# Transposing a head's two weight tiles together into two-bank PSUM tiles, and adding the causal mask on VectorE

## The chip, the cores and the metric

The kernel runs on one NeuronCore of a Trainium2 chip. The metric is the device time of one launch in microseconds (us). A core has five engines that run side by side and meet at semaphores: TensorE (PE in the profile; its weight loads are PEld), VectorE (DVE), ScalarE (ACT), GpSimd (POOL) and SyncE (SP), which only issues transfers. PSUM, the memory into which TensorE writes, has eight banks of 512 float32 values per partition; ScalarE and VectorE read it, GpSimd does not.

## The reference

One layer of a streaming encoder for 1024 prompt frames and 64 sample frames, width 1024, all in float32. What the change touches is the attention of the prompt, in two branches of eight heads (64 wide):

```
h = RMSNorm(x);  q, k, v of both branches, f, gate = h @ w_in;  q, k normalised per head
A: each 64-frame chunk reads itself and the 8 chunks before it
   p = softmax(q.k / 8 + bias[head, distance]);        o_a = p @ v
B: causal, c = cumsum(log sigmoid(f + b_f)) per head
   p = softmax(q.k / 8 + c[t] - c[s], s <= t);         o_b = p @ v
x = x + (sigmoid(gate_a) * (o_a @ w_pa) + sigmoid(gate_b) * (o_b @ w_pb)) @ w_o
x = x + experts(RMSNorm(x))     (32 experts, two of them per frame)
```

## The kernel before, in words

The frames are nine tiles of 128 (the last one holds the 64 sample frames). Every float32 product is made of float32r matmuls on a high and a low part, so a value that a matmul reads is first split: ScalarE copies it to float32r (the high part), VectorE subtracts that from the value (the low part).

The first 620 us or so are eight passes, one for each pair of heads: pairs 0 to 3 of branch A, then 0 to 3 of branch B. In a pass (`qkv`) TensorE projects the nine tiles with 24 matmuls a tile, and between these matmuls the attention of the pair is worked in, in four query groups `g` of 256 frames (two tiles `j` of 128), for two heads `h`. After it come gates, merges and the sample's heads, the output projection, and the experts, whose weights stream from HBM.

One head of one group goes like this. `scores(j)` multiplies q with up to 1024 keys into one or two PSUM tiles `big`; VectorE adds the bias (branch A) or `S = bias - c` (branch B) and keeps a running minimum (L598); ScalarE takes the exponential (L536), VectorE the reciprocal of the sum (L538), ScalarE scales (L540). In branch B one more bf16 matmul, identity times `tribig`, adds the causal mask to the last 128 columns. `weights(j, u)` transposes up to four 128x128 blocks of S (`tr`, L95) into a one-bank PSUM tile `small`; ScalarE copies it into `PT` as the high part (L635), VectorE subtracts for the low part (L636). So a tile j with more than four blocks in its group takes two such calls, u = 0 and 1. `values` then multiplies v with PT into another `small`. `turn_qk` transposes the normalised q and k of the next pair of frame tiles (`raw`) into a `small` too; three ScalarE instructions (L470, L474 twice) and two of VectorE (L475) read that one.

The order on TensorE is fixed by hand. Each call is put into a queue with a due time, either a number of ticks (a tick is three projection matmuls) or a time on a clock that the planner advances by its own estimate of TensorE's work (`late`). `D_W0 = 8` is the distance from a tile's scores to its first transposes, `D_W1 = 1.2` that from u = 0 to u = 1, `D_VAL = 4.5` that to `values`. TensorE takes its instructions strictly in that order: one that waits holds all behind it. Which buffer of a pool a tile gets, and the order on the other engines, a scheduler decides when the kernel is built. PSUM has two pools of four one-bank buffers: `big` (NBIG) and `small` (NSMALL). A tile of a pool can be written when the last reader of its buffer's former tile is done.

Of the kernel before, what the change touches and what calls it, by code (L numbers as in the profile page):

```python
# [24 lines left out]
CAP = 96  # L25
NOV = 22
EPS = 1e-6
NBIG, NSMALL = 4, 4
O_TURN, O_LOG, O_RANK, O_TAB = 3, 4, 7, 3
SA, SB, PTA, PTB, NORM_POOL, D_NORM, ATT0, ATT1, WPOOL, WR, SS, WO_EVERY, PF, SQ, FOX_POOL, V_POOL, RC_ACT, KT, NX, NN, NU0, E0, YB = 4, 3, 2, 1, 2, 0, 2, 26, 0, 4, 1, 3.5, 3, 2, 0, 2, 2, 1, 10, 1, 8, -1, 3  # L30
PA, PF2, HOLD_G, HELD, WARM0, XG, OT, HXB = 8, 2, -1, 1, 11, 3, 2, 1
# [4 lines left out]
NW, FPAIR, D_TURN, H_NORM, H_TURN, GRP = 16, 1, 10, 0, 4, 2  # L36
D_W0, D_W1, D_VAL, PACE = 8, 1.2, 4.5, 4.5
SL = [(0, 384), (384, 384), (768, 320)]
# [8 lines left out]
class K:  # L47
# [139 lines left out]
    def turn_h(self, i, k0):  # L187
        nc, x, n = self.nc, self.xs[i], rows(i)
        ps = self.pp.tile([128, 4, 128], F32, name="small", bufs=NSMALL)
# [74 lines left out]
    def forget(self):  # L264
# [45 lines left out]
        def sums():  # L310
            pc = self.pp.tile([128, 2, 104], F32, name="small", bufs=NSMALL)
            lff = lf.rearrange("p i h -> p (i h)")
# [13 lines left out]
        def store():  # L326
            pn = self.pp.tile([104, 128], F32, name="small", bufs=NSMALL)
# [242 lines left out]
    def scores(self, br, p, g, h, j, T, bias, G, H):  # L570
# [13 lines left out]
        if br == 1:  # L584
            (nc.gpsimd if FOX_POOL else nc.vector).tensor_scalar(
                S[:, :n], bias[h][:, :n], self.cc[:, i, 2 * p + h:2 * p + h + 1], None, op0=OP.subtract)
        pcs = self.pieces(n)
        for x, (o, m) in enumerate(pcs):
            ps = self.pp.tile([128, 512], F32, name="big", bufs=NBIG)
            ks = slice(128 * kb0 + o, 128 * kb0 + o + m)  # L590
            qs = slice(128 * j, 128 * j + 128)
            last = br == 1 and x == len(pcs) - 1
# [12 lines left out]
    def weights(self, br, p, g, h, j, T, G, H, u):  # L605

        nc = self.nc
        b0, nb = self.blocks(br, g)
        i = 2 * g + j
        kb0 = max(0, i - 4) if br == 0 else 0  # L610
        if u == 0:
            if nb > 4:
                self.late(D_W1, self.weights, br, p, g, h, j, T, G, H, 1)
        if j == 1 and u == (nb > 4):
            self.late(D_VAL, self.values, br, p, g, h, T, G, H)
        if ("PT", u) not in H:
            m, bufs = (2, self.pt_bufs) if u == 1 and nb == 6 else (4, 2)
            PT = H["PT", u] = self.ap_.tile([128, 2, m, 256], F32R, name=f"PT{m}", bufs=bufs)
            for b, jj in ((2 * g + 1, 0), (b0, 1)) if br == 0 and g >= 2 else ((2 * g + 1, 0),):
                uu, r = divmod(b - b0, 4)  # L620
                if uu == u:
                    nc.gpsimd.memset(PT[:, :, r, 128 * jj:128 * jj + 128].bitcast(F32), 0.0)
        PT = H["PT", u]
        r0, r1 = kb0 - b0, i - b0
        a, b = max(r0, 4 * u), min(r1, 4 * u + 3)
        if a > b:
            return
        S = H["S", j]
        pt = self.pp.tile([128, 4, 128], F32, name="small", bufs=NSMALL)
        for r in range(a, b + 1):  # L630
            c = (r - r0) * 128
            self.tr(pt[:, r - 4 * u, :], S[:, c:c + 128], self.ident)
        sr = slice(a - 4 * u, b + 1 - 4 * u)
        hi = PT[:, 0, sr, 128 * j:128 * j + 128]
        nc.scalar.copy(hi, pt[:, sr, :])  # L635
        nc.vector.tensor_tensor(PT[:, 1, sr, 128 * j:128 * j + 128], pt[:, sr, :], hi.bitcast(F32), op=OP.subtract)  # L636

    def values(self, br, p, g, h, T, G, H):
# [3 lines left out]
        at = G["at"]  # L642
        po = self.pp.tile([128, 256], F32, name="small", bufs=NSMALL)
        for r in range(nb):
            u, rr = divmod(r, 4)
            for hl in range(2):
                self.mm(po, T["v"][(b0 + r) // 4][:, (b0 + r) % 4, h, :], H["PT", u][:, hl, rr, :],
                                 start=(r == 0 and hl == 0), stop=(r == nb - 1 and hl == 1))
# [22 lines left out]
    def sample2(self, br, p, P, rk, rv, qk, qh, ql):  # L671
        nc, I = self.nc, self.I
        pt = self.pp.tile([128, 4, 128], F32, name="small", bufs=NSMALL)
        for i in range(4):
# [6 lines left out]
        def head(h):  # L681
# [15 lines left out]
            if br == 1:  # L697
                nc.vector.tensor_scalar(S, bias[:, :576], self.cc[:64, 12, hd:hd + 1], None, op0=OP.subtract)
            for x, o in enumerate((0, 288)):
                ps = self.pp.tile([128, 512], F32, name="big", bufs=NBIG)  # L700
                sl = slice(o, o + 288)
                last = br == 1 and x == 1
                self.mm(ps[:64, :288], qh[:, h], ks[h][:, sl], start=True, stop=False)
                self.mm(ps[:64, :288], ql[:, h], ks[h][:, sl], start=False, stop=not last)
                if last:
                    self.mm(ps[:64, 224:288], self.identb[:64, :64], self.tribig[:64, :64],
                                     start=False, stop=True)
                add = bias[:, sl] if br == 0 else S[:, sl]
# [6 lines left out]
        def weights(h, V, S):  # L715
            pt = self.pp.tile([128, 5, 64], F32, name="small", bufs=NSMALL)
            for i in range(5):
# [10 lines left out]
        def values(h, V, PT):  # L728
            rw = slice(64 * h, 64 * h + 64)
            po = self.pp.tile([128, 256], F32, name="small", bufs=NSMALL)  # L730
            for i in range(5):
# [168 lines left out]
    def out_tile(self, i, mh, ml):  # L900
# [5 lines left out]
        def turn(k0):  # L906
            pt = self.pp.tile([128, 4, 128], F32, name="small", bufs=NSMALL)
            for k in range(4):
# [28 lines left out]
        def logits():  # L937
            pl = self.pp.tile([128, 40], F32, name="small", bufs=NSMALL)
            for k in range(8):
# [67 lines left out]
    def place(self, i, n, OH, E):  # L1007

        nc = self.nc
        V = nc.vector  # L1010
        pp = self.pp.tile([128, 32], F32, name="small", bufs=NSMALL)
        for j in range(2):
# [58 lines left out]
    def turn(self, xg):  # L1071
# [3 lines left out]
        for k0 in (0, 4):  # L1075
            pt = self.pp.tile([128, 4, CAP], F32, name="small", bufs=NSMALL)
            for k in range(4):
# [4 lines left out]
    def hidden(self, u, xT):  # L1082
        nc = self.nc
        ph = self.pp.tile([128, 2, CAP], F32, name="small", bufs=NSMALL)
        for j in range(2):
# [73 lines left out]
    def overflow(self):  # L1159
# [7 lines left out]
        self.placed = None  # L1167
        pc = self.pp.tile([128, 32], F32, name="small", bufs=NSMALL)
        for j in range(2):
# [69 lines left out]
    def run(self):  # L1239
# [178 lines left out]
```

## Time and profile before

| | us |
|---|---|
| median of 3 runs (1242.94 to 1246.67) | 1245.81 |
| the profiled execution, device time | 1241.81 |
| its span, first to last instruction | 1240.0 |
| TensorE busy in the span | 1190.5 (96%) |
| VectorE, ScalarE, GpSimd busy | 788.6, 740.9, 314.9 |

Of the profiled execution 1.8 us lie outside its span. In a view by windows each row is a stretch, with the busy time of every engine and the number of instructions in brackets; TensorE's granted clock (PEclk, 1.00 is 2.4 GHz) stands behind. A view of groups gives count, total and mean time of instructions of one line and shape, and what the engine waited for before them. Records of matmuls overlap, since they are pipelined: how fast TensorE goes is read from the distance of the starts.

### The profile page before, as it was taken

What the parts mean: (1) busy time and instruction counts of PE and PEld (TensorE: products, weight loads), DVE (VectorE), ACT (ScalarE), POOL (GpSimd) and SP (SyncE); (2) the same over time, 40 slices, a digit from 0 to 9 for tenths busy, and PEclk for the clock granted to TensorE, in tenths of its full rate; (3) what the DMA queues carried; (4) which work ended last, traced back from release to release, by engine and by line L of the source; (5) the groups of instructions that cost most, each with busy time, mean ns of one, the idle gap of its engine ahead of it and who ended that gap; (6) DMA issues with size and microseconds to landing.
All of it is one profiled execution on the core that took longest, in us unless ns stands there. A gap on an engine that the chain in (4) does not pass through costs nothing. (4 is left out here: it accounts for less than half of the span.)

```text
span 1240.0 us, 22375 instructions
## 1 busy us (share of the span) xinstructions
PE 1190.5 (96%) x7677; PEld 1105.5 (89%) x7677; DVE 788.6 (64%) x2412; ACT 740.9 (60%) x1730; POOL 314.9 (25%) x469
## 2 busy tenths in 40 slices
PE   8999999999999999999999999999999989999993
PEld 6999999999889999899899889999988859999983
DVE  5667776767388887967467686318644444666543
ACT  5789998989498898988566443423233322333331
POOL 2643435352433434100000000000000013445421
PEclk9999999999999999999999999999999998999988
DMA  8112121222322131411233332214584458999995
GB/s 283 50 61 80 44 73 52 71 65 71 69 66 73 53 84 35 81 53 32 73 92 116 104 91 75 88 33 132 199 292 161 159 195 251 302 288 285 287 290 137
DMA packets 102538, 156.31 MB, mean 126 GB/s; under 512 B 13581, under 2 KB 77941, under 8 KB 102389
## 3 DMA queue, kind: packets, MB, share of 16 engines
q1 hardware_dynamic: 92789, 124.43, 32.6%
q0 software_dynamic: 7168, 21.50, 8.1%
q10 hardware_dynamic: 2464, 8.91, 1.9%
q8 instruction: 61, 1.00, 0.3%
q14 instruction: 56, 0.46, 0.1%
HBM read 122.08 MB, written 38.23 MB: 129 GB/s over the span
## 5 line engine op out<-in xcount | busy, mean ns | idle before, releaser
L83 PE MATMUL big<-w,hTh 128*128 128x384 f32 (+1 forms) x1152 | 324.3, 354 | 1.6 <-ACT hTh L193 0.7
L83 PEld LDWEIGHTS big<-w,hTh 128*128 128x128 f32 x1152 | 204.6, 189 | 6.2 <-DVE w L234 1.0
L83 PE MATMUL big<-hTh,w 128*128 128x384 f32 (+1 forms) x768 | 205.7, 336 | 0.0
L83 PE MATMUL big<-w,hTl 128*128 128x384 f32 (+1 forms) x512 | 173.6, 339 | 0.9 <-DVE hTl L194 0.9
L83 PEld LDWEIGHTS big<-hTh,w 128*128 128x128 f32 x768 | 138.6, 189 | 1.2
L83 PE MATMUL big<-hTl,w 128*128 128x384 f32 (+1 forms) x384 | 126.4, 329 | 0.0
L636 DVE TENSOR_TENSOR PT<-small,PT 128x512 fp32r<-128x512 f32 (+2 forms) x192 | 98.9, 520 | 21.1 <-ACT PT L635 19.2
L536 ACT ACTIVATE S<-S,mns 128x640 f32<-128x640 f32 (+7 forms) x128 | 94.3, 737 | 26.3 <-DVE mns L598 25.3
L83 PE MATMUL big<-ath,w 128*128 128x384 f32 (+1 forms) x384 | 99.4, 335 | 0.0
L540 ACT ACTIVATE S<-S,rc 128x640 f32<-128x640 f32 (+7 forms) x128 | 94.0, 736 | 7.8 <-DVE rc L538 6.9
L83 PEld LDWEIGHTS big<-w,hTl 128*128 128x128 f32 x512 | 97.0, 190 | 1.3 <-DVE hTl L194 1.2
L95 PE MATMUL small<-ident,S 128*128 128x128 f32 x528 | 89.3, 273 | 4.7 <-ACT S L540 2.6
L635 ACT CAST PT<-small 128x512 fp32r<-128x512 f32 (+2 forms) x192 | 85.1, 448 | 11.3 <-PE small L95 6.7
L83 PE MATMUL small<-PT,v 128*128 128x256 f32 x608 | 83.5, 283 | 0.0
L411 POOL TENSOR_TENSOR ssr<-ssa,mhalf 128x8 f32<-128x8 f32 (+1 forms) x40 | 61.2, 1531 | 72.6 <-DVE ssa L410 55.9
L83 PEld LDWEIGHTS small<-PT,v 128*128 128x128 f32 x608 | 79.3, 188 | 0.1
L83 PE MATMUL big<-wo,mh 128*128 128x512 f32 x288 | 75.9, 402 | 0.0
L95 PEld LDWEIGHTS small<-ident,S 128*128 128x128 f32 x528 | 65.0, 140 | 10.2 <-ACT S L540 3.8
L83 PEld LDWEIGHTS big<-hTl,w 128*128 128x128 f32 x384 | 72.9, 190 | 0.0
L83 PEld LDWEIGHTS big<-ath,w 128*128 128x128 f32 x384 | 69.0, 190 | 1.4
L83 PE MATMUL big<-k,qh 128*128 128x320 f32 (+3 forms) x192 | 64.4, 339 | 3.2 <-DVE mns L598 3.2
L449 POOL TENSOR_TENSOR v<-raw,v 128x128 fp32r<-128x128 f32 x64 | 31.2, 487 | 133.3 <-DVE v L448 125.9
(259 smaller groups left out, 2568.9 us busy)
## 6 DMA issues: line engine op xcount, KB each, us to landing
uo<-in_w SPq DMA_DIRECT2D x43, 512.0 KB
ux<-in_w SPq DMA_DIRECT2D x30, 512.0 KB
ur<-in_w SPq DMA_DIRECT2D x23, 512.0 KB
wraw<-in_w_pair SPq DMA_DIRECT2D x56, 192.0 KB
wraw<-in_w_in SPq DMA_DIRECT2D x32, 192.0 KB
atd<-at SPq DMA_DIRECT2D x32, 128.0 KB
bias<-ccd SPq DMA_DIRECT2D x8, 512.0 KB
y<-in_x_prompt SPq DMA_DIRECT2D x8, 512.0 KB
```

The source lines that it names most:

```text
L83: self.nc.tensor.matmul(out, a, b, start=start, stop=stop)
L95: self.nc.tensor.transpose(out, a, ident)
L411: nc.gpsimd.tensor_tensor(r[:n, :4 * c], a[:n, :4 * c], self.mhalf[:n, :4 * c], op=OP.pow)
L449: (nc.gpsimd if V_POOL & 2 else nc.vector).tensor_tensor(V[:, i, :, 64:128], src, V[:, i, :, 0:64].bitcast(F32), op=OP.subtract)
L536: nc.scalar.activation(S[:nq, :n], S[:nq, :n], AF.Exp, bias=mn[:nq], scale=-1.0, accum_out=sm[:nq])
L540: nc.scalar.activation(S[:nq, :n], S[:nq, :n], AF.Copy, scale=rc[:nq])
L635: nc.scalar.copy(hi, pt[:, sr, :])
L636: nc.vector.tensor_tensor(PT[:, 1, sr, 128 * j:128 * j + 128], pt[:, sr, :], hi.bitcast(F32), op=OP.subtract)
```

## The change

Five things are done together.

- `small` is split off into a pool of its own. During the eight passes it holds two tiles `turn` of two banks each (NTURN = 2) in place of four of one bank. `turn_h`, `turn_qk` and two small steps of the forget gate use it as well. After the passes it is opened again with four one-bank `small`.
- `weights` is called once for a head, 7 units after the scores of its second tile (D_W0 = 7). It transposes all blocks of tile 0 into one `turn`, all blocks of tile 1 into another, and each is read by one ScalarE copy (now L627) and one VectorE subtraction (L628). D_W1 is gone. PT is one tile for all blocks: two buffers in branch A, one in branch B.
- `values` writes into a `big`.
- The mask matmul is gone. VectorE makes `S = bias - c` for all but the last 128 columns as before, and for the last 128 one instruction makes `bias - c + tribig` (L592).
- Branch B has four S buffers in place of three, and one low part of q (`ql`) in place of two.

```diff
-NBIG, NSMALL = 4, 4
+NBIG, NSMALL, NTURN = 4, 4, 2
-SA, SB, ... = 4, 3, ...
+SA, SB, ... = 4, 4, ...
-D_W0, D_W1, D_VAL, PACE = 8, 1.2, 4.5, 4.5
+D_W0, D_VAL, PACE = 7, 4.5, 4.5
...
+    def turned_tile(self, k):
+        return self.ps_.tile([128, 8, 128], F32, name="turn", bufs=NTURN)[:, :k]
...
     def turn_qk(...):
-        pt = self.pp.tile([128, 2, 2, 128], F32, name="small", bufs=NSMALL)
+        pt = self.turned_tile(4).rearrange("p (j i) t -> p j i t", j=2)
...
     def open_ap(self, br):
-        self.q_lows(self.ap_, 256, 2)
+        self.q_lows(self.ap_, 256, 2 - br)
...
     def scores(...):
         if br == 1:
-            (nc.gpsimd if FOX_POOL else nc.vector).tensor_scalar(
-                S[:, :n], bias[h][:, :n], self.cc[:, i, 2 * p + h:2 * p + h + 1], None, op0=OP.subtract)
+            c = self.cc[:, i, 2 * p + h:2 * p + h + 1]
+            if i:
+                nc.vector.tensor_scalar(S[:, :n - 128], bias[h][:, :n - 128], c, None, op0=OP.subtract)
+            nc.vector.scalar_tensor_tensor(S[:, n - 128:n], bias[h][:, n - 128:n], c, self.tribig,
+                                           op0=OP.subtract, op1=OP.add)
...
-            self.mm(ps[:, :m], ql[:, h, qs], K[:, ks], start=False, stop=not last)
-            if last:
-                self.mm(ps[:, m - 128:m], self.identb, self.tribig, start=False, stop=True)
+            self.mm(ps[:, :m], ql[:, h, qs], K[:, ks], start=False, stop=True)
...
-        self.late(D_W0, self.weights, br, p, g, h, j, T, G, H, 0)
+        if j == 1:
+            self.late(D_W0, self.weights, br, p, g, h, T, G, H)
...
+    def weights(self, br, p, g, h, T, G, H):
         nc = self.nc
         b0, nb = self.blocks(br, g)
+        self.late(D_VAL, self.values, br, p, g, h, T, G, H)
+        PT = H["PT"] = self.ap_.tile([128, 2, self.wide // 128 + 1 - br, 256], F32R, name="PT", bufs=self.pt_bufs)
...
+        for j in range(2):
+            i = 2 * g + j
+            kb0 = max(0, i - 4) if br == 0 else 0
+            r0, n = kb0 - b0, i + 1 - kb0
+            S = H["S", j]
+            pt = self.turned_tile(n)
+            for r in range(n):
+                self.tr(pt[:, r, :], S[:, 128 * r:128 * r + 128], self.ident)
+            hi, lo = (PT[:, x, r0:r0 + n, 128 * j:128 * j + 128] for x in range(2))
+            nc.scalar.copy(hi, pt)
+            nc.vector.tensor_tensor(lo, pt, hi.bitcast(F32), op=OP.subtract)
     def values(...):
-        po = self.pp.tile([128, 256], F32, name="small", bufs=NSMALL)
+        po = self.pp.tile([128, 512], F32, name="big", bufs=NBIG)[:, :256]
...
-            self.close("ap", "tp")
+            self.close("ap", "tp", "ps")
+            self.ps_ = self.open("ps", 1, PSUM)
```

The sample's heads lose their mask matmul in the same way; the other lines of the diff only name the new pool.

How the change moves instructions on TensorE is seen at two places. A number behind a name tells one buffer's tile from the next; the brackets name the engines on whose semaphores an instruction waits. First, branch A, pair 1, group 2, second head. Before, the first three blocks of its second tile (small_2468), then the q and k of the next frame tiles (small_2474), then, after three projection matmuls, the last two blocks (small_2494):

```order
L95 MATMUL small_2468<-ident_72,S_2313 128x128 [waits PE_49]
L95 MATMUL small_2468<-ident_72,S_2313 128x128 x2
L95 MATMUL small_2474<-ident_72,raw_2178 128x128 [waits DVE_49,PE_49,Pool_49]
L95 MATMUL small_2474<-ident_72,raw_2178 128x128 [waits Pool_49]
L95 MATMUL small_2474<-ident_72,raw_2178 128x128 x2
L83 MATMUL big_2388<-w_1675,hTh_91 128x384
L83 MATMUL big_2487<-w_1525,hTh_91 128x384
L83 MATMUL big_2487<-w_1525,hTl_92 128x384
L95 MATMUL small_2494<-ident_72,S_2313 128x128 [waits DVE_49]
L95 MATMUL small_2494<-ident_72,S_2313 128x128
```

Now, the five blocks of tile 0 (turn_2418), the five of tile 1 (turn_2426) and the q and k (turn_2434) stand without anything between them:

```order
L83 MATMUL big_2361<-w_1621,hTh_91 128x384
L99 MATMUL turn_2418<-ident_72,S_2225 128x128 x5
L99 MATMUL turn_2426<-ident_72,S_2285 128x128 [waits Activation_49]
L99 MATMUL turn_2426<-ident_72,S_2285 128x128 x4
L99 MATMUL turn_2434<-ident_72,raw_2145 128x128 [waits DVE_49,Pool_49]
L99 MATMUL turn_2434<-ident_72,raw_2145 128x128 [waits Pool_49]
L99 MATMUL turn_2434<-ident_72,raw_2145 128x128 x2
L83 MATMUL big_2361<-w_1639,hTh_91 128x384
```

There are two `turn` buffers, so turn_2434 has the buffer of turn_2418; the wait on DVE in front of it is for the subtraction that reads turn_2418, five transposes earlier.

Second, branch B, pair 1, group 3, second head, its second tile. Before, the mask matmul and the eight blocks in two halves with projection between them:

```order
L83 MATMUL big_6661<-tribig_82,identb_80 128x128
L95 MATMUL small_6671<-ident_72,S_6531 128x128 [waits DVE_49]
L95 MATMUL small_6671<-ident_72,S_6531 128x128 x3
L83 MATMUL big_6568<-w_6215,hTh_91 128x384
L83 MATMUL big_6568<-w_6215,hTl_92 128x384
L83 MATMUL big_6568<-w_6218,hTh_91 128x384
L83 MATMUL big_6568<-w_6221,hTh_91 128x384
L83 MATMUL big_6691<-w_6070,hTh_91 128x384
L83 MATMUL big_6691<-w_6070,hTl_92 128x384
L95 MATMUL small_6705<-ident_72,S_6531 128x128 [waits DVE_49]
L95 MATMUL small_6705<-ident_72,S_6531 128x128 x3
```

Now, seven blocks of tile 0 and at once the eight of tile 1:

```order
L83 MATMUL big_6403<-w_6066,hTh_91 128x384
L99 MATMUL turn_6494<-ident_72,S_6302 128x128 [waits PE_49]
L99 MATMUL turn_6494<-ident_72,S_6302 128x128 x6
L99 MATMUL turn_6504<-ident_72,S_6373 128x128 [waits DVE_49,PE_49]
L99 MATMUL turn_6504<-ident_72,S_6373 128x128 x7
L83 MATMUL big_6403<-w_6081,hTh_91 128x384
L83 MATMUL big_6525<-w_5926,hTh_91 128x384
L83 MATMUL big_6525<-w_5926,hTl_92 128x384
```

Here the scheduler has put both tiles, turn_6494 and turn_6504, into the same two banks, and the wait on DVE in front of the second is for the subtraction that reads the first. Such a pair in one buffer stands at 13 of the 64 heads (five with 1 block in tile 0, three with 3, three with 5, two with 7), and q and k right behind both tiles of a head, as in the first place, seven times, all in branch A.

## Rows read from the trace of the kernel before

**Rows 1.** The page's first part: busy time of each engine.
```profile
PE 1190.5 (96%) x7677; PEld 1105.5 (89%) x7677; DVE 788.6 (64%) x2412; ACT 740.9 (60%) x1730; POOL 314.9 (25%) x469
```

**Rows 2.** Stretches, one per pass of a pair: span, busy by engine, clock, DMA.
```profile
184.00:246.00 62.00, 61.39 (x407) 59.84 (x406) 44.77 (x139) 56.02 (x133) 26.50 (x45) 1.00 0.20 60
...
459.00:528.00 69.00, 66.79 (x448) 62.96 (x447) 57.04 (x173) 62.38 (x150) 20.25 (x34) 1.00 0.26 59
...
sum 537.00, PE 526.93 PEld 501.48 DVE 402.11 ACT 465.30 POOL 185.07; mean PE 65.87 PEld 62.69 DVE 50.26 ACT 58.16 POOL 23.13
```

**Rows 3.** TensorE's waits, 31 to 620 us: for whom, us, times, longest.
```profile
PE big L83 <- DVE mns L598: 3.2, 4, 1.8
PE small L95 <- ACT S L540: 2.6, 3, 1.8
...
PE small L95 <- ACT qk L464: 1.0, 1, 1.0
PE small L95 <- DVE PT L636: 1.0, 2, 0.6
```

**Rows 4.** Timeline of TensorE, branch B: start, us, instruction.
```profile
438.16 0.34 PE L83 MATMUL big<-w,hTl 128*128 128x384 f32 x1
438.34 0.34 PE L83 MATMUL big<-w,hTh 128*128 128x384 f32 x1
...
440.95 0.23 PE L83 MATMUL big<-tribig,identb 128*128 128x128 bf16 x1
440.99 0.59 PE L83 MATMUL big<-w,hTh 128*128 128x384 f32 x2
441.42 0.34 PE L83 MATMUL big<-w,hTl 128*128 128x384 f32 x1
```

**Rows 5.** Groups by shape, 31 to 620 us: count, busy us, mean ns, idle before.
```profile
L636 DVE TENSOR_TENSOR PT<-small,PT 128x512 fp32r<-128x512 f32 x72 | 49.4, 687 | 12.7 <-ACT PT L635 12.0
L635 ACT CAST PT<-small 128x512 fp32r<-128x512 f32 x72 | 42.0, 583 | 7.1 <-PE small L95 4.6 <-PE small L83 1.7
...
L475 DVE SCALAR_TENSOR_TENSOR k<-small,k 64x256 fp32r<-64x256 f32 x64 | 30.9, 483 | 11.4 <-ACT k L474 9.8
...
L474 ACT ACTIVATE k<-small 64x256 fp32r<-64x256 f32 x64 | 29.8, 465 | 3.1 <-DVE k L475 2.3
...
L213 DVE SCALAR_TENSOR_TENSOR w<-wraw,small,w 128x128 fp32r<-128x128 f32 x62 | 19.0, 347 | 4.0 <-ACT w L212 3.7
...
L636 DVE TENSOR_TENSOR PT<-small,PT 128x128 fp32r<-128x128 f32 x40 | 11.3, 284 | 1.4 <-ACT PT L635 1.1
L635 ACT CAST PT<-small 128x128 fp32r<-128x128 f32 x40 | 10.3, 257 | 0.3
...
L585 DVE TENSOR_SCALAR S<-bias,cc 128x1024 f32<-128x1024 f32 x8 | 6.2, 769 | 0.4 <-PE small L95 0.4
...
L585 DVE TENSOR_SCALAR S<-bias,cc 128x128 f32<-128x128 f32 x8 | 2.6, 319 | 7.8 <-DMA bias<-ccd 7.4 <-PE small L95 0.3
```

**Rows 6.** Timeline of a four-block transposition whose readers were free.
```profile
466.08 0.61 PE L95 MATMUL small<-ident,S 128*128 128x128 f32 x4
...
466.44 0.42 PE L83 MATMUL big<-w,hTh 128*128 128x384 f32 x1
...
466.70 0.34 PE L83 MATMUL big<-w,hTl 128*128 128x384 f32 x1
466.72 0.59 ACT L635 CAST PT<-small 128x512 fp32r<-128x512 f32 x1 [1.38 <-PE small L95]
...
467.34 0.69 DVE L636 TENSOR_TENSOR PT<-small,PT 128x512 fp32r<-128x512 f32 x1 [0.63 <-ACT PT L635]
```

**Rows 7.** Timeline of a four-block transposition whose readers were occupied.
```profile
432.43 0.66 PE L95 MATMUL small<-ident,S 128*128 128x128 f32 x4 [1.02 <-ACT qk L464]
...
434.20 0.57 ACT L635 CAST PT<-small 128x512 fp32r<-128x512 f32 x1
...
435.34 0.68 DVE L636 TENSOR_TENSOR PT<-small,PT 128x512 fp32r<-128x512 f32 x1
```

More of the change, by code (lines that the diff above doesn't have):

```diff
@@ L188, in turn_h @@
         nc, x, n = self.nc, self.xs[i], rows(i)
-        ps = self.pp.tile([128, 4, 128], F32, name="small", bufs=NSMALL)
+        ps = self.turned_tile(4)
         for k in range(4):
@@ L310, in sums @@
         def sums():
-            pc = self.pp.tile([128, 2, 104], F32, name="small", bufs=NSMALL)
+            pc = self.turned_tile(2)[:, :, :104]
             lff = lf.rearrange("p i h -> p (i h)")
@@ L326, in store @@
         def store():
-            pn = self.pp.tile([104, 128], F32, name="small", bufs=NSMALL)
+            pn = self.turned_tile(1)[:104, 0]
             self.tr(pn, ccf, self.ident)
@@ L602, in scores @@
         self.softmax(mns[:, x:x + 1], S, n, 128, j < RC_ACT)
-        self.late(D_W0, self.weights, br, p, g, h, j, T, G, H, 0)
-    def weights(self, br, p, g, h, j, T, G, H, u):
+        if j == 1:
+            self.late(D_W0, self.weights, br, p, g, h, T, G, H)
+    def weights(self, br, p, g, h, T, G, H):
         nc = self.nc
         b0, nb = self.blocks(br, g)
[L609 to L636, printed above, removed]
@@ new lines, in weights @@
+        self.late(D_VAL, self.values, br, p, g, h, T, G, H)
+        PT = H["PT"] = self.ap_.tile([128, 2, self.wide // 128 + 1 - br, 256], F32R, name="PT", bufs=self.pt_bufs)
+        for b, jj in ((2 * g + 1, 0), (b0, 1)) if br == 0 and g >= 2 else ((2 * g + 1, 0),):
+            nc.gpsimd.memset(PT[:, :, b - b0, 128 * jj:128 * jj + 128].bitcast(F32), 0.0)
+        for j in range(2):
[9 more added lines that the diff above has]
+            nc.vector.tensor_tensor(lo, pt, hi.bitcast(F32), op=OP.subtract)
@@ L672, in sample2 @@
         nc, I = self.nc, self.I
-        pt = self.pp.tile([128, 4, 128], F32, name="small", bufs=NSMALL)
+        pt = self.ps_.tile([128, 4, 128], F32, name="small", bufs=NSMALL)
         for i in range(4):
@@ L697, in head @@
             if br == 1:
-                nc.vector.tensor_scalar(S, bias[:, :576], self.cc[:64, 12, hd:hd + 1], None, op0=OP.subtract)
+                c = self.cc[:64, 12, hd:hd + 1]
+                nc.vector.tensor_scalar(S[:, :512], bias[:, :512], c, None, op0=OP.subtract)
+                nc.vector.scalar_tensor_tensor(S[:, 512:], bias[:, 512:576], c, self.tribig[:64, :64],
+                                               op0=OP.subtract, op1=OP.add)
             for x, o in enumerate((0, 288)):
@@ L701, in head @@
                 sl = slice(o, o + 288)
-                last = br == 1 and x == 1
                 self.mm(ps[:64, :288], qh[:, h], ks[h][:, sl], start=True, stop=False)
[L704 to L707, printed above, removed]
+                self.mm(ps[:64, :288], ql[:, h], ks[h][:, sl], start=False, stop=True)
                 add = bias[:, sl] if br == 0 else S[:, sl]
@@ L715, in weights @@
         def weights(h, V, S):
-            pt = self.pp.tile([128, 5, 64], F32, name="small", bufs=NSMALL)
+            pt = self.ps_.tile([128, 5, 64], F32, name="small", bufs=NSMALL)
             for i in range(5):
@@ L729, in values @@
             rw = slice(64 * h, 64 * h + 64)
-            po = self.pp.tile([128, 256], F32, name="small", bufs=NSMALL)
+            po = self.ps_.tile([128, 256], F32, name="small", bufs=NSMALL)
             for i in range(5):
@@ L906, in turn @@
         def turn(k0):
-            pt = self.pp.tile([128, 4, 128], F32, name="small", bufs=NSMALL)
+            pt = self.ps_.tile([128, 4, 128], F32, name="small", bufs=NSMALL)
             for k in range(4):
@@ L937, in logits @@
         def logits():
-            pl = self.pp.tile([128, 40], F32, name="small", bufs=NSMALL)
+            pl = self.ps_.tile([128, 40], F32, name="small", bufs=NSMALL)
             for k in range(8):
@@ L1010, in place @@
         V = nc.vector
-        pp = self.pp.tile([128, 32], F32, name="small", bufs=NSMALL)
+        pp = self.ps_.tile([128, 32], F32, name="small", bufs=NSMALL)
         for j in range(2):
@@ L1075, in turn @@
         for k0 in (0, 4):
-            pt = self.pp.tile([128, 4, CAP], F32, name="small", bufs=NSMALL)
+            pt = self.ps_.tile([128, 4, CAP], F32, name="small", bufs=NSMALL)
             for k in range(4):
@@ L1083, in hidden @@
         nc = self.nc
-        ph = self.pp.tile([128, 2, CAP], F32, name="small", bufs=NSMALL)
+        ph = self.ps_.tile([128, 2, CAP], F32, name="small", bufs=NSMALL)
         for j in range(2):
@@ L1167, in overflow @@
         self.placed = None
-        pc = self.pp.tile([128, 32], F32, name="small", bufs=NSMALL)
+        pc = self.ps_.tile([128, 32], F32, name="small", bufs=NSMALL)
         for j in range(2):
@@ L1285, in swap @@
                 return
-            self.close("ap", "tp")
+            self.close("ap", "tp", "ps")
+            self.ps_ = self.open("ps", 1, PSUM)
             self.atp = self.open("atp", 1)
```

6 lines of the change are left out of this document (2 added, 4 removed).

## The prediction

> **What bounds the kernel now.** I read the page's busy times first: TensorE is busy 96% of the span, no other engine more than 64% [rows 1]. A share over the whole span hides stages, so next came the view by stretches, one per pass of a head pair, since all of the change lies in those passes. There TensorE is busy 526.93 of 537 us at the full clock, 2.4 GHz (1.00); ScalarE comes second with 56.02 of 62 us in a pass of branch A and 62.38 of 69 in one of branch B [rows 2]. So TensorE sets the pace, with 10 us of gaps in eight passes, and whatever makes it stand still there is added to the end; the stages behind follow its order and shift with it. Third, the view of waits: none of the causes of these gaps is above 3.2 us, and only 2.0 us are waits for a PSUM buffer of transposes to be read (for L464 and L636) [rows 3]. The reader is to see that PSUM costs almost nothing now, although its readers ScalarE and VectorE are loaded.
>
> **The mask.** Without a mask matmul, two projection passes take 2 x 0.18 us (438.16 to 438.34); with one ahead, it takes from 440.95 to 441.42 until two passes are through, so the mask costs 0.11 to 0.12 [rows 4]. 64 of them give 7.0 us, the sample's eight smaller ones 0.5 at most: 7.5 us off TensorE's path. The number of transposes stays 528, and four of them take 466.08 to 466.70 less one pass, 0.11 each, with no visible price for starting a group [rows 6]; fusing calls saves TensorE nothing.
>
> VectorE takes the mask over. The new form, two tensors and a scalar on 128 columns, has its nearest row in L213 (347 ns); 128 columns less of L585 give back (769 - 319) / 7 = 64 ns [rows 5]. 56 tiles at 0.28 us and eight that only change form at 0.03 make 16 us in branch B. Fewer evictions give some of it back: one block costs 257 ns on ScalarE and 284 on VectorE, four cost 583 and 687, so the part that doesn't grow is 0.15 us on each [rows 5], and 64 fewer in both branches save 9.6 us on each engine, half of that in branch B. VectorE has 57.04 busy of 69 us there [rows 2]; (16 - 4.8) / 4 = 2.8 more per pass still fits beside TensorE. I cost it at nothing by itself; where its queue stands in the way it is in the delays below.
>
> **The two `turn` buffers.** This is the large term. The evictions are not on TensorE's path while another buffer is free. In the new order they are: 13 times the second tile of a head is transposed into the very banks of the first, and seven times q and k follow five transposes after the tile whose buffer they need. There TensorE waits until ScalarE has copied and VectorE has subtracted the whole first tile; behind it in its queue stand the projection passes that nothing else holds.
>
> The price from rows: TensorE can go on at 466.08 + 4 x 0.11 = 466.52, the copy starts at 466.72 and the subtraction ends at 468.03 [rows 6]. So beside the two instructions 0.25 us pass. With 0.148 + 0.109 per block on ScalarE and 0.150 + 0.134 on VectorE [rows 5] a tile of 1, 3, 5 or 7 blocks is free 0.79, 1.28, 1.76 or 2.25 us after its last transpose. Same buffer: 5 x 0.79 + 3 x 1.28 + 3 x 1.76 + 2 x 2.25 = 17.6 us. Behind both: 7 x (1.76 - 0.55) = 8.5 us. Together 26.1 us with nothing in the readers' queues.
>
> The readers do have queues. The same four blocks that took 1.51 us in one place took 432.87 to 436.02 in another, 1.6 us more [rows 7]. Bounds for each of the 20 places are therefore 0 and 1.6. I take 0.8, the middle: ScalarE has nine tenths of its time taken, but each halt of TensorE also stops the feeding of these queues. That adds 16 us. In 12 more places a buffer is needed 1.0 to 2.1 us of TensorE's work after its last write: four in branch A (q and k 1.5 us after three blocks, 0.55 short at 0.8 of queue), six in branch B (one at 1.0, 1.1 short; the others hardly short), and two where four blocks follow q and k by 1.56 us (3 x 465 + 483 ns and 0.25, 2.1 us [rows 5], so 1.4 short). That is 6.5 us, between 1.4 with empty queues and 16 with 1.6 us of queue.
>
> So the buffers cost 48.6 us, between 27.5 and 74; about 28 of it in branch A, 20 in branch B.
>
> On larger evictions the Trainium skill (Perfetto Trace Analysis, Optimizing Scalar/DVE Operations) speaks both ways: grouping into larger operations helps if the engine is saturated, and "If Scalar/Vector aren't saturated, but are causing bubbles on other engines, breaking up instructions may allow work to be completed sooner." By the first the 9.6 us saved on ScalarE would count, which is one of the rivals below; by the second only the bubbles do, which is the sum here.
>
> **Smaller terms.** The 2.0 us of waits for transposes' buffers now [rows 3] are replaced: minus 2. `values` joins the four `big`, where score tiles waited 3.2 us before [rows 3]: between minus 3 and plus 10, and I take plus 3, near the row. `values` starts 4.5 units after the first transposes; in the largest heads some 3.3 us of TensorE's work is left after the last of them, and eight blocks need 0.25 + 1.02 + 1.22 = 2.5, so 0.8 of queue just fits: 0, with 1.6 of queue 0.6 us at eight heads and some of the next size, 8 us at most. I take 1. The first transposes come one unit nearer to the scores; waits for the scaled S were 2.6 us [rows 3], and a stopped TensorE gives ScalarE time, so I take no change, between minus 3 and plus 10. The single `ql` and the single PT of branch B are written after their last reader, which the order puts about a quarter of a head ahead; no charge, in the bounds of the last terms.
>
> **The sum.** -7.5 + 48.6 - 2 + 3 + 1 = +43 us. The profiled execution took 1241.81 us, 1.8 outside its span, so it becomes 1285. It lay 4.0 us under the median of the runs, 1245.81; against that 43 us make about 1289. I say 1288. Low end of all bounds: -7.5 + 27.5 - 2 - 3 - 3 = +12, 1258. High end: -7.5 + 74 - 2 + 10 + 8 + 10 = +92, 1338.
>
> **Rivals.**
> - The queues are empty when it matters: halts let ScalarE and VectorE catch up, and only the evictions' own time is paid. That is the low end, 1258. For it: rows 6 show such a place. Against it: ScalarE's nine tenths.
> - Faster: ScalarE is the pace in the full stretches and the buffers are no matter, because TensorE would have come late to these places anyway. Then the mask (7.5) and the fused evictions (9.6) count, 1229. It decides this way if the 20 places cost under 0.4 us each on average; the smallest of them needs 0.79 by the rows, and TensorE's gaps before were only 10 us in all, so little can be won.
> - VectorE becomes the bound in branch B: its 2.8 us a pass more come in front of score tiles whose `big` buffers now turn round faster, and every late reading stops TensorE. Then the high end, 1338. For it: 57 of 69 us busy before. Against it: longer passes dilute it.
> - No change: halts of about 8 us in all pay for the mask exactly, 1246. Nothing in the rows makes them that short.
>
> **How the numbers follow.** Halts with some queue: 0.70, own range 1268 to 1312. Empty queues: 0.13. VectorE as the bound: 0.08. Faster: 0.06. No change: 0.03. The range 1255 to 1322 takes in the first case, the greater part of the second and the beginning of the third. A measurement tells 0.3% (about 4 us) from no change; faster by that 0.06, within 0.04, slower 0.90.
>
> **What the profile after would show.** The waits of TensorE from 31 us to the end of the passes have `turn` behind the subtraction L628 as the first row, with 25 to 60 us, in place of 1.0; each of the 13 pairs shows a gap in front of the second tile's transposes of at least 0.6 us. ScalarE's copies of seven blocks take 0.9 us, VectorE's subtractions 1.1. No mask matmul; L592 takes 0.30 to 0.35 us. Passes of branch A grow by some 7 us each, those of branch B by 3 or so; everything from the gates to the end keeps its length, within 3 us. It is wrong if the waits for L628 are under 15 us, if the passes of branch B get shorter, or if the time after them changes by more than the passes do.

## The result, and the profile after

The changed kernel takes 1332.77 us (median of 4 runs, 1328.36 to 1333.52), the kernel before 1244.79 beside it: 1.0699 times as long, 95% interval 1.0669 to 1.0729. The forecast was 1288 us with a range to 1322: slower was right, but the change costs 88 us and not 43. The profiled execution took 1333.5 us, 1.8 of them outside its span.

The page's first line answers [rows 1]: TensorE is busy 18.7 us longer although it has 72 fewer recorded matmuls, and yet its share of the span falls from 96% to 91%.

```profile
PE 1209.2 (91%) x7605; PEld 1126.0 (85%) x7605; DVE 800.7 (60%) x2412; ACT 743.3 (56%) x1666; POOL 310.4 (23%) x467
```

The stretches of [rows 2], now with the bounds of whole passes (two of branch A, pairs 1 and 2 of branch B, and the last pass; columns as there):

```profile
217.00:288.60 71.60, 63.65 (x408) 61.68 (x406) 44.20 (x132) 55.98 (x124) 26.75 (x45) 0.98 0.18 53
288.60:359.60 71.00, 63.41 (x406) 61.68 (x405) 41.95 (x120) 51.63 (x109) 24.27 (x43) 0.98 0.16 50
462.60:547.40 84.80, 70.86 (x427) 67.21 (x426) 58.31 (x162) 60.44 (x124) 23.38 (x39) 0.94 0.23 52
547.40:625.30 77.90, 67.58 (x429) 63.95 (x428) 58.77 (x174) 62.39 (x141) 16.07 (x29) 0.98 0.23 56
625.30:685.40 60.10, 59.97 (x404) 58.61 (x401) 44.66 (x132) 48.00 (x104) 3.08 (x12) 1.00 0.13 36
```

Two things have changed. TensorE stands still for 7.6 to 13.9 us in a pass, where it did so for 0.6 to 2.2 before. And the granted clock, 1.00 throughout before, is 0.94 to 0.98. Neither is so in the last pass, whose order has no q and k to turn: there the two tiles of a head always get different buffers.

The waits of TensorE in the passes (for whom; us in total, times, longest) answer [rows 3]:

```profile
PE turn L99 <- DVE PT L628: 42.6, 23, 3.9
PE turn L99 <- DVE k L479: 15.7, 7, 3.8
PE turn L99 <- DVE rc L542: 6.4, 3, 2.6
PE big L83 <- DVE mns L602: 5.5, 6, 1.5
```

The three rows with `turn` are 64.7 us; before, transposes waited 2.0 us for their buffers. (The row of rc L542 is three of the same places: VectorE's reciprocal ends there 0.07 to 0.16 us behind the subtraction L628 that the buffer waits for.) The price of a tile's reading is as forecast from [rows 5]: 0.15 and 0.134 us a block make 0.82 us for five blocks on VectorE, and ScalarE's copy stays under its 0.70; the mask's instruction is a little dearer than the 0.30 to 0.35 forecast.

```profile
L628 DVE TENSOR_TENSOR PT<-turn,PT 128x640 fp32r<-128x640 f32 x40 | 31.9, 819 | 12.3 <-ACT PT L627 12.2
...
L627 ACT CAST PT<-turn 128x640 fp32r<-128x640 f32 x40 | 26.3, 692 | 2.4 <-PE turn L99 1.9
...
L592 DVE SCALAR_TENSOR_TENSOR S<-bias,cc,tribig 128x128 f32<-128x128 f32 x64 | 24.2, 378 | 11.6 <-DMA bias<-ccd 9.6 <-PE turn L99 1.8
```

The next rows are a halt of the kind forecast, in the timeline (start, us, engine and instruction; in brackets the idle time before it). Seven blocks, then the eight of the second tile into the same two banks; they answer [rows 6]:

```profile
451.44 0.93 PE L99 MATMUL turn<-ident,S 128*128 128x128 f32 x7
...
452.46 0.91 ACT L627 CAST PT<-turn 128x896 fp32r<-128x896 f32 x1 [0.29 <-PE turn L99]
...
453.40 1.09 DVE L628 TENSOR_TENSOR PT<-turn,PT 128x896 fp32r<-128x896 f32 x1 [0.64 <-ACT PT L627]
...
454.63 1.58 PE L99 MATMUL turn<-ident,S 128*128 128x128 f32 x8 [2.27 <-DVE PT L628]
```

The copy comes 0.1 us after the last transposes, takes 0.91, the subtraction 1.09: 2.27 us of TensorE, with hardly any queue. The next rows are the same with a queue, as in [rows 7]: a tile of one block, whose reading takes 0.27 and 0.29 us, holds TensorE for 3.93, because ScalarE still has an exponential, a scaling and an older q and k in front of it.

```profile
385.23 0.27 PE L99 MATMUL turn<-ident,S 128*128 128x128 f32 x1
...
386.06 0.71 ACT L540 ACTIVATE S<-S,mns 128x512 f32<-128x512 f32 x1
...
387.13 0.46 ACT L478 ACTIVATE k<-turn,small 64x256 fp32r<-64x256 f32 x1
...
387.88 0.72 ACT L544 ACTIVATE S<-S,rc 128x512 f32<-128x512 f32 x1
...
388.63 0.27 ACT L627 CAST PT<-turn 128x128 fp32r<-128x128 f32 x1
...
388.99 0.29 DVE L628 TENSOR_TENSOR PT<-turn,PT 128x128 fp32r<-128x128 f32 x1 [0.32 <-POOL ssr L415]
...
389.43 0.41 PE L99 MATMUL turn<-ident,S 128*128 128x128 f32 x2 [3.93 <-DVE PT L628]
```

What I had not counted on is the clock. The next rows are the stretch of the first halt above, the 3.4 us behind it, and the next 3.4 (columns as in [rows 2]): in the last two TensorE is busy all the time, but has 15 matmuls in the one and 25 in the other.

```profile
451.40:454.60 3.20, 0.97 (x9) 0.69 (x7) 2.07 (x6) 1.91 (x4) 0.00 (x0) 1.00 0.00 0
455.00:458.40 3.40, 3.40 (x15) 3.40 (x14) 1.65 (x3) 2.03 (x3) 0.00 (x0) 0.50 0.00 0
458.40:461.80 3.40, 3.40 (x25) 3.40 (x24) 1.36 (x7) 1.05 (x4) 2.01 (x2) 0.99 0.14 43
```

A granted clock of 0.50 is TensorE's 1.2 GHz; its matmuls of 384 columns start 0.32 us apart there (456.65, 456.97, 457.29) and 0.17 to 0.18 behind it. Such a stretch of 3.4 us stands twelve times between 31 and 686 us, and each begins in a halt of 2.27 to 3.93 us or at most 1.4 us behind its end; before, there was none between 14 and 618 us.

The account of the time in the two profiled executions, summed over the idle times in front of TensorE's instructions and the stretches at half clock, up to the last matmul of the merges and from there to the end:

| us | before | after |
|---|---|---|
| last matmul of the merges | 883.6 | 964.9 |
| gaps of TensorE, 31 us to there | 16.6 | 82.1 |
| stretches at 1.2 GHz in that time | 6.8 | 47.8 |
| rest (time from 31 us on, less gaps, less half the stretches) | 832.5 | 827.8 |
| from there to the end | 356.5 | 366.8 |
| gaps / stretches in it | 13.4 / 27.9 | 19.5 / 37.0 |

So 65.5 us of the growth are gaps, 20.5 half clock (half of 41.0 us), minus 4.7 work; and 10.3 come behind the merges. (The end of the last pass would not do as a mark: that pass is 4.0 us shorter, mainly because 20 recorded projection matmuls fewer stand in it, 3.5 us; they now come behind it.)

### The profile page after: what moved, and what is told of

Its sections match the earlier page's. It is cut to its first block, busy times and chain, and to the rows that moved or that the text cites. A ratio compares the mean times of both kernels' runs of the same rounds, so it can differ in the third digit from the quotient of the medians.

```text
span 1331.7 us, 22131 instructions
## 1 busy us (share of the span) xinstructions
PE 1209.2 (91%) x7605; PEld 1126.0 (85%) x7605; DVE 800.7 (60%) x2412; ACT 743.3 (56%) x1666; POOL 310.4 (23%) x467
## 4 chain that ended last, share of the span: by engine, by line
PE 48%; DMA 12%; DVE 7%; ACT 4%; issue 2%; POOL 0%; SPq 0%; ACTq 0%; DVEq 0%; POOLq 0%
PE big L83 37%; PE small L83 6%; DMA ur<-in_w 4%; PE small L99 3%; DMA uo<-in_w 2%; DMA ux<-in_w 2%; PE turn L99 2%; DVE S L602 1%; DVE PT L628 1%; DVE S L591 1%; DMA bias<-ccd 1%; DMA out_y<-y 1%; ACT S L540 1%; DMA wraw<-atd 1%; DVE S L592 1%
## 5 line engine op out<-in xcount | busy, mean ns | idle before, releaser
L83 PEld LDWEIGHTS big<-w,hTh 128*128 128x128 f32 x1152 | 214.2, 196 | 5.8 <-ACT w L231 1.3
L83 PE MATMUL big<-hTh,w 128*128 128x384 f32 (+1 forms) x768 | 202.4, 334 | 0.0
L83 PE MATMUL big<-w,hTl 128*128 128x384 f32 (+1 forms) x512 | 177.2, 346 | 0.6 <-DVE hTl L198 0.6
L99 PE MATMUL turn<-ident,S 128*128 128x128 f32 x528 | 74.8, 280 | 47.1 <-DVE PT L628 26.2
L99 PEld LDWEIGHTS turn<-ident,S 128*128 128x128 f32 x528 | 61.8, 143 | 53.4 <-issue 28.0
L628 DVE TENSOR_TENSOR PT<-turn,PT 128x640 fp32r<-128x640 f32 (+7 forms) x128 | 87.8, 702 | 22.8 <-ACT PT L627 21.7
L83 PEld LDWEIGHTS big<-w,hTl 128*128 128x128 f32 x512 | 100.3, 196 | 1.1 <-DVE hTl L198 0.8
L83 PE MATMUL big<-PT,v 128*128 128x256 f32 x608 | 86.6, 288 | 5.1 <-DVE mns L602 3.0
L83 PEld LDWEIGHTS big<-PT,v 128*128 128x128 f32 x608 | 81.0, 192 | 8.1 <-issue 3.7
L627 ACT CAST PT<-turn 128x640 fp32r<-128x640 f32 (+7 forms) x128 | 72.9, 599 | 18.7 <-PE turn L99 14.2
```

The lines of the kernel that those rows point to most:

```text
L83: self.nc.tensor.matmul(out, a, b, start=start, stop=stop)
L99: self.nc.tensor.transpose(out, a, ident)
L627: nc.scalar.copy(hi, pt)
L628: nc.vector.tensor_tensor(lo, pt, hi.bitcast(F32), op=OP.subtract)
```

## The experiments

**1. q and k out of the `turn` buffers.**

```diff
-        pt = self.turned_tile(4).rearrange(...)
+        pt = self.pp.tile([128, 512], F32, name="big", bufs=NBIG).rearrange(...)
```

> The changed kernel, with one line undone: the transposes of q and k go into a one-bank `big` memory, so that only the weights use the two `turn` buffers; their tiles then alternate, and no tile stands nearer than 3.6 us of TensorE's work behind the last write of its own buffer (in the changed kernel 13 stand at 0). Theory (TensorE halts because a `turn` buffer is asked for before VectorE has subtracted its last tile, and the halts drop its clock): the waits for the subtraction of PT fall from 42.6 us to under 4, those for the subtraction of k (15.7) go, the 12 stretches at 1.2 GHz in the passes go; 1333 less 65 us of gaps less 20 us of half clock, plus 5 to 15 for more waits at `big`: 1250 to 1265. Rival (VectorE and ScalarE are overloaded by the larger evictions and the mask, and the buffers only show it): the waits move to `big`, 1300 or more.

1266.61 us, ratio to before 1.0154 (1.0117 to 1.0192), 1.6 us above the expected range. The passes lose 63 of the 78 us by which they had grown. The waits of TensorE up to 690 us (columns as above) hold no buffer of weights any more:

```profile
PE big L83 <- DVE mns L602: 10.2, 9, 2.9
PE big L99 <- DVE mns L602: 4.2, 4, 2.1
...
PE big L83 <- DVE PT L628: 1.7, 4, 0.6
```

Gaps up to the merges are 33.5 us instead of 82.1, stretches at 1.2 GHz 17.1 instead of 47.8. The theory holds in the waits for L628 and for k; but 13.7 us of stretches at half clock are left in the passes, where it expected none. What is left is score tiles read late, nearly all in branch B.

**2. One-bank pieces.** The pieces have up to four blocks, in four buffers; both tiles still go at once (the helper `turned_tile` is written out here).

```diff
-            pt = self.turned_tile(n)
-            for r in range(n):
+            for a in range(0, n, 4):
+                m = min(4, n - a)
+                pt = self.ps_.tile([128, 4, 128], F32, name="small", bufs=NSMALL)[:, :m]
```

> The changed kernel with the two-bank memories alone undone: both tiles of a head are still transposed in one go, but in pieces of up to four blocks into four one-bank buffers, which q and k share as before. Theory: a buffer is free after four blocks (1.5 us) and another three are there; 11 places still stand closer than 0.8 us to the last write of their buffer (four of weights, seven of q and k), at 0.9 plus a queue of 0.8 us each some 18 us; less the mask's 7.5: 1250 to 1265, and at most two stretches at half clock in the passes. Rival (transposing both tiles in one go is the cause, whatever the memories): 1300 or more.

1269.61 us, 1.0179 (1.0141 to 1.0218), 5 over the expectation; the waits for the subtraction fall from 42.6 us to the row below. Seven of its eleven are q and k right behind the two tiles, 10.3 us, and four stretches at half clock are left, not two. So without the two-bank memories 63 of the 88 us are gone. Experiment 1 kept them and took back 66: the two edits remove the same halts and can't be added.

```profile
PE small L99 <- DVE PT L630: 15.9, 11, 2.0
```

**3. The mask alone**, in the kernel before (with the sample's heads alike):

```diff
...
-                S[:, :n], bias[h][:, :n], self.cc[...], None, op0=OP.subtract)
+                S[:, :n - 128], bias[h][:, :n - 128], c, None, op0=OP.subtract)
+            nc.vector.scalar_tensor_tensor(S[:, n - 128:n], bias[h][:, n - 128:n], c, self.tribig,
+                                           op0=OP.subtract, op1=OP.add)
...
-                self.mm(ps[:, m - 128:m], self.identb, self.tribig, start=False, stop=True)
```

> The kernel before with the mask alone moved to VectorE (in the passes and in the sample). Theory (the mask matmul is on TensorE's path, VectorE's 2.8 us more per pass of branch B lie beside it): 7.5 us less, given back 0 to 3: 1237 to 1241. Rival (VectorE becomes the bound in branch B): 1250 or more, all of the difference in the passes of branch B.

1238.14 us, 0.9942 (0.9918 to 0.9965): 7 us saved, as costed. This is the version that beats both kernels.

**4. Work in the halts.** In front of the second tile's transposes of twelve heads:

```diff
+            if j and (br, p, g, h) in FILL:
+                self.warm(9)
```

> The changed kernel with nine matmuls of 512 columns without a reader put in front of the second tile's transposes at those twelve heads whose halt was followed by a stretch at 1.2 GHz; buffers and order of everything else stay. They take 1.9 us of halts of 2.3 to 3.9 us. Theory (the clock falls because TensorE stands still, and each stretch of 3.4 us at half clock costs 1.7 us): the halt places take as long as before, the clock stays at 2.4 GHz in the passes, 12 x 1.7 = 20 us less: about 1313. Rival (the stretches at 1.2 GHz cost nothing, because TensorE waits for VectorE anyway): 1330 to 1335 although the clock stays up.

1320.85 us, 1.0604 (1.0558 to 1.0649). The matmuls fit into the halts, whose rows shrink by about their 23 us:

```profile
PE turn L101 <- DVE PT L632: 28.4, 24, 2.0
PE turn L101 <- DVE k L481: 9.8, 7, 2.6
...
PE turn L101 <- DVE rc L544: 3.2, 2, 2.6
```

Four stretches at half clock are left in the passes. One follows a filled place, the tile of one block shown above: there TensorE still stood for 2.01 us behind the nine matmuls. The other three are at other places, two of them behind halts of 2.61 and 2.05 us that had none in the changed kernel. The twelve were 41 us, these are 13.7, and half of the difference, 13.7, stands against 10.8 us by which the passes got shorter. The clock is a cost of its own, then, and its size is right; at eleven of the twelve places the halt need not even be gone, it was enough that TensorE worked in it.

**5. The second tile 1.2 us of TensorE's work behind the first**, two-bank memories kept.

```diff
-        for j in range(2): ...
+        self.weights_of(br, g, 0, H)
+        self.late(D_W1, self.weights_of, br, g, 1, H)      # D_W1 = 1.2
```

> The changed kernel with the second tile's transposes 1.2 us of TensorE's work behind the first's; two-bank memories, two buffers and all else stay. 8 tiles still have their predecessor's buffer, but 1.3 to 1.9 us of projection now lies between. Theory (a halt is the time of reading a tile, 0.25 us and the two instructions and about 1.1 us of queue, less the work that lies between): some 25 to 30 us of halts are left of 65, and most stretches at 1.2 GHz go: 1275 to 1295. Rival (two buffers are too few wherever the tiles stand): 1315 or more.

1291.97 us, 1.0371 (1.0337 to 1.0406): as expected, 41 us given back by projection work put between two tiles. But 19.2 us of the gaps are now `values` that wait for PT, since the second tile moved towards them:

```profile
PE big L83 <- DVE PT L632: 12.5, 19, 1.5
...
PE big L83 <- ACT PT L631: 6.7, 5, 2.4
```

**6. The mask back on TensorE** in the changed kernel (the edit of experiment 3, reversed).

> The changed kernel with the mask alone given back to TensorE (64 mask matmuls in the passes, eight in the sample; VectorE subtracts the plain bias). Theory (the mask is worth its matmuls and nothing else): 7 us more, 1338 to 1342. Rival (VectorE's added 2.8 us per pass of branch B lengthen the halts there): less than now, below 1330, with shorter passes in branch B.

1325.43 us, 1.0643 (1.0603 to 1.0683, overlapping the interval of the changed kernel a little): not slower. The theory is wrong for this kernel. The last matmul of the merges ends at 964.0 us against 964.9; the 64 mask matmuls are paid by gaps that are 6.2 us shorter in sum (75.9 against 82.1), all in branch B, where VectorE has less work in front of the readings:

```profile
PE turn L99 <- DVE PT L628: 35.8, 20, 3.9
PE turn L99 <- DVE k L479: 15.3, 7, 4.5
PE turn L99 <- DVE rc L542: 9.5, 4, 2.5
```

The rest of the difference lies behind the merges (358.7 us against 366.8), where the code is the same; more on it below.

**7 and 8. The values out of `big`**, on top of experiment 2, and then the spacing of experiment 5 as well.

```diff
-        po = self.pp.tile([128, 512], F32, name="big", bufs=NBIG)[:, :256]
+        po = self.ps_.tile([128, 256], F32, name="small", bufs=NSMALL)
```

> The changed kernel with one-bank pieces in four shared buffers, and the result of the values back in these, out of `big`. What is left of the change is the order in one go, the joined PT and single ql of branch B, and the mask. Theory (values in `big` cost score tiles their buffer, about 10 us in branch B): 1256 to 1266, the waits for the score readings L602 at 3 us, as in the kernel before; what is left over the mask alone are some 20 places where one-bank buffers are asked for within 1.5 us of their last write. Rival (values in `big` cost nothing; VectorE reads the scores late because of its own load): 1270 as with one-bank pieces alone, or more.

> The kernel of one-bank pieces with the values in the same buffers, and the second tile 1.2 us of TensorE's work behind the first: no buffer is asked for within 1.6 us of its last write. What is left of the change is the mask, the joined PT, the single ql of branch B and the first transposes at 7 instead of 8 units. Theory (the order and the PSUM buffers are all that cost time): within 4 us of the mask alone, 1236 to 1243. Rival (the single PT or ql of branch B hold up the next head): 1250 or more, with waits in branch B for PT or ql.

Seven: 1269.25 us, 1.0196 (1.0163 to 1.0229), the same as experiment 2. The waits for the score readings do fall, from 6.8 to 3.2 us, but those for the four shared buffers rise from 15.9 to 23.1: `values` in `big` cost nothing on balance, and my theory was wrong. Eight: 1268.88 us, 1.0205 (1.0177 to 1.0233), missed by 26. The waits show why; the first and the third row are `values`, 18.2 us, as in experiment 5:

```profile
PE small L83 <- DVE PT L634: 13.2, 22, 1.5
PE small L99 <- DVE PT L634: 7.1, 3, 3.1
PE small L83 <- ACT PT L633: 5.0, 5, 2.6
```

**9 to 11. The values 1.2 us later too** (`D_VAL` 5.7 instead of 4.5): with one-bank pieces, with the two-bank memories, and with these and q and k in `big`.

> The last kernel (one-bank pieces, values in the same buffers, second tile 1.2 us behind the first) with the values 1.2 us later, so that they again stand 4.5 us of TensorE's work behind the second tile's transposes, as in the kernel before. There, 18 of its 30 us of gaps were values that waited for PT. Theory (those waits came from that edit's own timing): they fall under 4 us, 18 us and about 3 of half clock less: 1243 to 1250. Rival (the single PT of branch B, which the copies can write only when the head before has been multiplied, holds them up): branch B keeps its 14 us of such waits, 1258 or more.

> The two-bank kernel with the second tile 1.2 us behind the first, and now with the values 1.2 us later too. Of its 46 us of gaps in the passes 19 were values that waited for PT. Theory: these go, the 20 us of waits for `turn` buffers stay: 1268 to 1276. Rival (later values hold PT and S longer and the waits only move): 1285 or more.

> The same two-bank kernel with q and k out of the `turn` buffers, in `big`. Theory (with no `turn` buffer asked for early, only the score tiles' waits for `big` are left, 16 us in the first experiment): 1255 to 1265. Rival (`big` now carries too much, and its waits take back what the spacing gives): 1268 or more, not better than the first experiment's 1267.

Nine: 1252.68 us, 1.0083 (1.0061 to 1.0105). The waits of `values` are gone; 3 us over the expectation, since new places came up:

```profile
PE small L99 <- DVE PT L634: 11.1, 9, 4.1
PE small L99 <- DVE k L479: 5.9, 2, 3.2
...
PE small L83 <- DVE PT L634: 0.9, 3, 0.3
```

So in this version the single PT and `ql` of branch B hold up nothing that can be seen. Ten: 1283.72 us, 1.0340 (1.0313 to 1.0368), between theory and rival: of the 19 us, 16 go, but the waits for `turn` behind VectorE's subtraction rise from 8.4 to 20.9. Eleven: 1258.08 us, 1.0133 (1.0105 to 1.0161), as expected. With both remedies the two-bank memories still are slower than the kernel before, whose mask matmuls this version doesn't have.

Not tried alone: the first transposes one unit nearer to the scores, and the fourth S buffer of branch B. They are in experiment 9 too, which is 14.5 us slower than the mask alone (1238.14); up to the merges its gaps are 10.8 us longer (29.7 against 18.9).

The account holds for all of them: from 31 us up to the merges, time less gaps less half of the stretches at 1.2 GHz is 824 to 833 us in twelve of the thirteen profiles (852 with the filling matmuls of experiment 4), while the gaps run from 16.6 to 82.1. Behind the merges it is 326 to 330.

## Why the forecast had the sign and half the size

**Right: the halts.** The 13 pairs in one buffer halted TensorE each, by 2.52, 1.51, 1.12, 1.12 and 3.93 us (one block), 3.44, 2.50 and 2.50 (three), 3.02, 2.60 and 2.59 (five), 2.27 and 2.27 (seven): 31.4 us where the forecast had 17.6 and 13 x 0.8 = 28.0. Less the 17.6 this leaves 1.06 us of queue in each instead of 0.8. The seven q and k behind both tiles took 12.1 us where it had 14.1. So the 20 places were 43.5 for 42.1, and the waits for L628 were the first row, with 42.6 us, as foretold. (That row is not just these places: 6.4 us of the 20 stand in the row of L542, and five other waits, 5.4 us, in that of L628.)

**Mis-sized: the "12 more places".** They had 6.5 us; the rest of the `turn` waits is 64.7 - 43.5 = 21.2. The step that failed is the reading of q and k: I priced "two where four blocks follow q and k" with 2.1 us of instructions, less 1.56 of distance, and 0.8 of queue; the 2.1 are three instructions of ScalarE and one of VectorE. But there are two of VectorE, and the five go from ScalarE to VectorE, back, and to VectorE again, each time into another queue. The rows show one such reading:

```profile
570.03 0.49 PE L99 MATMUL turn<-ident,S 128*128 128x128 f32 x3
...
571.80 0.48 DVE L479 SCALAR_TENSOR_TENSOR k<-turn,small,k 64x256 fp32r<-64x256 f32 x1
572.31 0.49 DVE L591 TENSOR_SCALAR S<-bias,cc 128x512 f32<-128x512 f32 x1
572.31 0.47 ACT L478 ACTIVATE k<-turn,small 64x256 fp32r<-64x256 f32 x1 [0.68 <-DVE k L479]
572.71 0.34 DVE L592 SCALAR_TENSOR_TENSOR S<-bias,cc,tribig 128x128 f32<-128x128 f32 x1
572.98 0.61 DVE L602 CUSTOM_DVE_ANT_0 S<-big,S,mns 128x384 f32<-128x384 f32 x1
...
573.70 0.49 DVE L479 SCALAR_TENSOR_TENSOR k<-turn,small,k 64x256 fp32r<-64x256 f32 x1
...
574.34 0.95 PE L99 MATMUL turn<-ident,S 128*128 128x128 f32 x4 [3.82 <-DVE k L479]
```

The four transposes of q and k had started at 568.33, and the three of tile 0 went into the other buffer. VectorE does the first half of k at 571.80, ScalarE the second at 572.31 (it waited for VectorE), and VectorE's turn for that comes at 573.70, behind the bias, the mask and a score reading. TensorE stands still for 3.82 us. Four such places cost 2.60, 2.29, 3.29 and 3.82 us and three with two blocks 1.11, 1.28 and 1.26: 15.7 us in the row of L479. Experiment 1, which takes q and k out, removes this row and the 13 pairs together; this row alone was not tried. The remaining 5.4 us are five waits of q and k in branch B for L628, of 0.83 to 1.39 us.

**Failed: the full clock.** The forecast read "the full clock, 2.4 GHz" in [rows 2] and costed halts at their own length. Twelve stretches at 1.2 GHz added 20.5 us. Experiment 4 shows that this is a cost and not a by-product. The Trainium skill (TensorE: Matmul & The Clock Gate, A second HAM failure mode: psum-queue depth-cycling) tells of a like case: TensorE idles briefly between groups of matmuls as it cycles through PSUM buffers, and its clock goes down and up. The trace agrees in kind, with twelve stretches at 0.50. The Trainium skill (TensorE: Matmul & The Clock Gate, HAM oscillation — how this bites in real kernels) counts the loss, in a kernel that waits for transfers, as half of the throttled time. The trace agrees: 0.32 us against 0.175 a matmul, and in experiment 4 10.8 us for the 13.7 that half of the stretches gone would be.

**Failed: "everything from the gates to the end keeps its length".** 10.3 us came behind the merges: 6.1 in gaps and 4.6 in half clock, less 0.4, by the table. One gap can be followed. In the changed kernel one issue of a transfer by ScalarE took 3.32 us; the copy behind it, and with it TensorE, came late:

```profile
977.42 3.32 ACTq L918 DMA_DIRECT2D out_y<-y  x1
...
980.78 0.59 ACT L900 COPY yT<-small 128x512 f32<-128x512 f32 x1 [2.69 <-issue]
...
981.42 1.09 PE L83 MATMUL small<-wr,yT 128*128 128x40 f32 x8 [1.34 <-ACT yT L900]
```

In the kernel before the issue at this place took 0.39 us, and the longest 0.54. The profiles of experiments 1 and 4 have one of 3.28 and of 4.08 us, the other nine none over 0.54, among them experiment 6, whose code is the same there. So the code at that place alone does not make it. But each kernel has one profile, and all four runs of the changed kernel (1328 to 1334 us) lie above all four of experiment 6 (1320 to 1327): that the time behind the merges is an event of single executions, and not the change, is not shown. What held the issue, and the other gaps and half clock of the expert stage, stay open.

**The mask.** Minus 7.5 us was right where TensorE does not wait (experiment 3) and worth nothing, up to the merges, where it does (experiment 6: 0.9 us the other way, with one profile of each). The rival with VectorE as the bound in branch B gave nearly the right time, 1338, for another reason: 59.3 of the 65.5 us of added gaps are there without its mask, too (75.9 - 16.6), and only 6 us come from it. Empty queues, no change and faster are out: the queue was longer than the 0.8 us taken. The other terms held: waits for `big` were 5.5 us for 3.2 (forecast plus 3), `values` in it cost nothing on balance (experiment 7), and the single PT and `ql` nothing in experiment 9. The passes of branch A grew by 8 to 12 us (forecast 7), the first three of branch B by 10 to 17 (forecast 3).

In the changed kernel itself the single PT, for which the forecast had no charge, did hold ScalarE up twice, by 2.08 and 0.88 us: by the profile its copies waited for the `values` of the head before, themselves late behind the halts of 3.29 and 3.82 us. The next q and k on TensorE then waited 1.39 and 1.07 us, two of the five waits above. The first of the two:

```profile
491.59 0.97 ACT L627 CAST PT<-turn 128x384 fp32r<-128x384 f32 x2 [2.08 <-PE big L83]
...
493.85 0.31 PE L99 MATMUL turn<-ident,raw 64*128 64x64 f32 x2 [1.39 <-DVE PT L628]
```

Put together: of gaps the forecast had 48.6 - 2 + 3 + 1 = 50.6 and 65.5 came, 14.9 more; 20.5 of half clock, 10.3 behind the merges and 2.8 by which the work shrank less (4.7, not 7.5). With the 43.1 forecast this makes 91.6; the span grew by 91.7.

## What to carry to other kernels

Count PSUM buffers not by banks but by how long one is held: from the last write over all its readers, with what stands in their queues, against the work that lies before the next write; five instructions on two engines held one here longer than two on a tile of seven blocks. Add to a halt of TensorE what its clock loses afterwards, 1.7 us here behind twelve of fourteen halts of 2.3 to 3.9 us, and fill a halt that can't be removed with work. And a saving on TensorE counts only where TensorE doesn't wait: the same mask was worth 7 us in one kernel and none in the other.

## What the hardware showed unexpectedly

Of the 14 halts of 2.27 us or more in the passes 12 went with 3.4 us at 1.2 GHz; filling these with matmuls that nobody reads kept the clock up at eleven of them. Such stretches stood behind shorter halts, too: in experiment 2 behind four of 1.81 to 2.03 us. One issue of a transfer on ScalarE's queue took 3.3 to 4.1 us in three of thirteen profiles, and 0.34 to 0.54 us elsewhere; each time it was the first of the nine of `out_y`.
